# Seven products for seven of a layer's eight up blocks, with two of four weight sums made by accumulating transfers

## The chip, the cores and the metric

One NeuronCore of a Trainium2 chip runs the whole program. The metric is the device time of one execution in microseconds; lower is better. TensorE multiplies into PSUM, ScalarE and VectorE work on SBUF and PSUM, GpSimd (POOL) on SBUF, and the queues of SyncE (SP) and POOL start transfers from memory (HBM).

## The reference

A decoder trunk of two layers over 256 tokens with 2048 features, everything in float32. Each layer has an attention, a cross-attention into 256 memory tokens, and an MLP, each with an RMS norm ahead and a residual add behind. The change lies in the MLP, which is more than half of the work:

```python
def sq_relu_mlp(h, wup, wdown):
    return jnp.square(jax.nn.relu(h @ wup)) @ wdown        # wup 2048 x 8192, wdown 8192 x 2048

x = x + sq_relu_mlp(rms_norm(x, mlp_norm[i]), mlp_wup[i], mlp_wdown[i])
```

## The kernel before, in words

**Products.** TensorE takes float32 operands rounded to a shorter form, so each operand is kept as two parts, a high part and the rest, and each product is three matmuls: high by high, high by rest, rest by high. The activations stand still (128 x 128), the weights move (128 x 512). Activations are split once per layer stage, weights each time they are loaded.

**The path of a weight.** Weights come in tiles of 128 x 2048 floats (1024 KB) into one of RAWS = 6 raw buffers, by SP's queue. A tile is an item: `split_pieces` cuts it into two halves of 128 x 1024, ScalarE casts each to `whi` (L193), VectorE subtracts to get `wlo` (L194). whi and wlo have four buffers each, so two items' halves. TensorE then multiplies (all matmuls are recorded at L155). A raw buffer is free again when its second wlo is made; a whi or wlo buffer when TensorE has used that half.

**The MLP.** The hidden features come in eight blocks of 1024 (`MLP_BLOCKS`), each of two halves of 512. There are three kinds of item:

- an up item: one tile of `wup` by both token tiles (t = 0, 1), 24 matmuls of 512 columns; eight of them make a block;
- a down item: one tile of `wdown` by both token tiles, 24 matmuls, sums in PSUM that are added to the residual x at L439; four columns groups (c = 0 to 3) of two items for each block;
- a product item: one of the seven products of a block, half of its 16 row groups (x = 0, 1), 12 matmuls.

The seven products are Winograd's form of Strassen's rule for a 2 x 2 partition: the activations as a11 to a22 (token tile by half of the features), the block's weights as b11 to b22 (half of the features by half of the hidden columns). Seven products with sums of four forms of the activations (`s1` to `s4`, made once per layer by `Forms.sums`) and four sums of weight tiles take the place of eight. A block of up items has 2 x 4 x 24 = 192 matmuls, a block by seven products 14 x 12 = 168. Six blocks of a layer go by seven products (`SEVEN` = 1, 2, 3, 5, 6, 7), blocks 0 and 4 by up items.

`Seven.job` makes the weights of an item: it loads a tile, or adds tiles in raw buffers on VectorE at 128 x 2048 each. Before, the sums are p5 (L748, t = b12 - b11), p6 (L752, t = b22 - t), p7 (L757, t - b11) and p4 (L762, t - b21), each for x = 0 and 1, so eight a block. `Seven.products` multiplies, copies a finished product out of PSUM or adds it to another (`add`, L790, "evacuation" below), and passes the sums to `out`, which squares them on ScalarE, transposes them on TensorE and splits them for the down items.

**The order.** TensorE's order is written out: `mlp_line` mixes the items of seven products with the others (`rest`). It keeps a `lead`, the load of the items placed so far less their share by TensorE's time, and takes a product item where the lead is spent or a down item's hidden tiles are not there yet. The orders of VectorE, ScalarE, POOL and SP follow from a schedule that is made when the program is built; from then on each engine goes through its own fixed list, and waits in it. Loads are planned four items ahead (`AHEAD`), and a load waits in SP's list for its raw buffer.

Of the kernel before, what the change touches and what calls it, by code (L numbers as in the profile page):

```python
# [14 lines left out]
ALU = mybir.AluOpType  # L15
# [6 lines left out]
CH = 512  # L22
EPS = 1e-6
WARM = 13
RAWS = 6
MLP_BLOCKS = 8
SEVEN = (1, 2, 3, 5, 6, 7)
EVS = 7

T_EV, T_TURN, T_ROT, T_SM, T_SQ, T_ADD, T_NORM = 2.6, 2.6, 12.0, 6.5, 4.4, 2.2, 6.5  # L30
# [15 lines left out]
def trunk(ctx, tc, x, xT, mem, memT, positions, gcols, gfinal, lam_vecs, consts, W, out):  # L46
    nc = tc.nc

    def pool(name, bufs, space=None):
        kw = {"space": space} if space else {}  # L50
        return ctx.enter_context(tc.tile_pool(name=name, bufs=bufs, **kw))

    keep = pool("keep", 1)
    wraw = pool("wraw", RAWS)
    whalf = pool("whalf", 4)
    units = pool("units", 13)
    work = pool("work", 2)
    small = pool("small", 3)
    banks = pool("banks", 8, bass.MemoryType.PSUM)
# [104 lines left out]
    def load(dst, src, queue=None):  # L164
        tc.keep_in_program_order((queue or nc.sync).dma_start(dst, src))
# [4 lines left out]
    def raw_tile():  # L170
        return wraw.tile([P, 4 * CH], F32, tag="raw", name=nm("raw"))
# [25 lines left out]
    def halves_of(raw, n=4 * CH, pieces=2):  # L197
        split = split_pieces(raw, n, pieces)
        for _ in range(pieces):
            split.next()  # L200
        return split.halves
# [166 lines left out]
    class Forms(Stream):  # L368
# [34 lines left out]
        def sums(self):  # L403
            for key in [(t, h) for t in range(NT) for h in range(2)]:
                for task in self.forms[key].tasks:
                    yield task
            for x in range(2):
                a11, a12, a21, a22 = (self.raw[t][:, 8 * h + 4 * x : 8 * h + 4 * x + 4] for t in range(NT) for h in range(2))
                for key, o, p, q, op in (
                    ("s1", a22, a21, a22, ALU.add), ("s3", a21, a11, a21, ALU.subtract),  # L410
                    ("s2", a22, a22, a11, ALU.subtract), ("s4", a12, a12, a22, ALU.subtract),
                ):
                    nc.vector.tensor_tensor(o, p, q, op)
                    self.halves(key, x, o)
                yield T_TURN
# [290 lines left out]
    class Chunk:  # L706
# [11 lines left out]
        def items(self):  # L718
            return [Item(self, u, [job]) for u, job in enumerate(self.all)]
# [5 lines left out]
    class Seven:  # L725


        ORDER = "p1 p1 p5 p5 p6 p3 p6 p3 p7 p7 p2 p4 p2 p4".split()
        A = {"p1": (0, 0), "p2": (0, 1), "p3": "s4", "p4": (1, 1), "p5": "s1", "p6": "s2", "p7": "s3"}

        def __init__(self, l, b):
# [1 line left out]
            self.raw = {}  # L733
            self.banks = {}

        def fetch(self, i, j, x):
            raw = raw_tile()
            load(raw, W[f"mlp_wup{self.l}"][4 * (2 * self.b + j) + 2 * i + x])
            return raw

        def job(self, p, x):
            def run():
                r = self.raw
                if p == "p1":
                    r[11, x] = o = self.fetch(0, 0, x)
                elif p == "p5":
                    r["t", x] = o = self.fetch(0, 1, x)
                    nc.vector.tensor_tensor(o, o, r.pop((11, x)), ALU.subtract)  # L748
                elif p == "p6":
                    r[22, x] = self.fetch(1, 1, x)  # L750
                    o = r["t", x]
                    nc.vector.tensor_tensor(o, r[22, x], o, ALU.subtract)  # L752
                elif p == "p3":
                    o = r.pop((22, x))
                elif p == "p7":
                    o = self.fetch(0, 0, x)
                    nc.vector.tensor_tensor(o, r["t", x], o, ALU.subtract)  # L757
                elif p == "p2":
                    r[21, x] = o = self.fetch(1, 0, x)
                else:  # L760
                    o = r.pop(("t", x))
                    nc.vector.tensor_tensor(o, o, r.pop((21, x)), ALU.subtract)  # L762
                return halves_of(o)

            return run

        def items(self):
            order = [(p, self.ORDER[:i].count(p)) for i, p in enumerate(self.ORDER)]
            return [Item(self, u, [self.job(*u)]) for u in order]

        def products(self, a, u, copied, out):
            p, x = u
            form = a.form(self.A[p])
            need(form.tasks)
            if x == 0:
                self.banks[p] = bank("pr")
            o = self.banks[p]
            for h, (hi, lo) in enumerate(take()):
                for k in range(2):
                    kk = 4 * x + 2 * h + k  # L780
                    wh, wl = (w[:, k * CH : (k + 1) * CH] for w in (hi, lo))
                    mmul(o, form[:, 0, kk], wh, kk == 0, False)
                    mmul(o, form[:, 0, kk], wl, False, False)
                    mmul(o, form[:, 1, kk], wh, False, kk == 7)
                pump()
            if x == 0:
                return

            def add(o, p, q, op=ALU.add):
                nc.vector.tensor_tensor(o, p, q, op)  # L790

            c = copied
            if p in ("p1", "p5", "p6", "p3"):
                c[p] = work.tile([P, CH], F32, tag="ev", name=nm(p), bufs=EVS)
            if p in ("p1", "p5"):
                nc.scalar.copy(c[p], o)
            elif p == "p6":
                add(c[p], o, c["p1"])
            elif p == "p3":
                add(c[p], o, c["p5"])  # L800
                add(c[p], c[p], c["p6"])
                out(0, 1, c[p], c[p])
            elif p == "p7":
                add(c["p6"], o, c["p6"])
                add(c["p5"], c["p6"], c["p5"])
                out(1, 1, c["p5"], c["p5"])
            elif p == "p2":
                add(c["p1"], o, c["p1"])
                out(0, 0, c["p1"], c["p1"])
            else:  # L810
                add(c["p6"], c["p6"], o, ALU.subtract)
                out(1, 0, c["p6"], c["p6"])

    def mlp_line(l):

        def up(b, h):
            return Chunk(l, "up", [(b, h)]).items()

        def both(b, *more):
            return [(b, 0), (b, 1), *more]

        groups = [both(0), both(1, (4, 0)), both(2), both(3, (4, 1)), both(5), both(6), both(7)]

        def down(i):


            end = len(groups) - 1
            pairs = ((0, 1), (2, 3)) if (end - i) % 2 == 0 else ((2, 3), (0, 1))  # L830
            chunks = [Chunk(l, "down", groups[i], c, open=i in (0, 2)) for c in pairs[0]]
            chunks += [Chunk(l, "down", groups[i], c, close=i in (1, end)) for c in pairs[1]]
            return [i for c in chunks for i in c.items()]

        line = up(0, 0)
        rest = up(0, 1) + up(4, 0) + down(0) + down(1) + up(4, 1) + down(2) + down(3) + down(4) + down(5)
        seven = [i for b in SEVEN for i in Seven(l, b).items()]

        def vector(item):

            if isinstance(item.of, Seven):
                p, x = item.u
                return 2 + 2 * (p in ("p5", "p6", "p7", "p4")) + x * {"p6": 0.55, "p3": 1.65, "p7": 1.65, "p2": 1.1, "p4": 1.1}.get(p, 0)
            return 2 + 1.1 * (item.u == len(item.of.all) - 1 and item.of.close)

        def tensor(item):
            return 1 if isinstance(item.of, Seven) else 2

        rest, after = rest[:-3], rest[-3:]

        share = sum(map(vector, rest + seven)) / sum(map(tensor, rest + seven))
        usable = {(0, 0): 0}
        lead, now = 6.0, 0
        while rest or seven:
            of = rest[0].of if rest else None
            late = rest and of.kind == "down" and any(usable.get(h, math.inf) > now for h in of.halves)
            take_seven = seven and (not rest or late or lead <= 0)
            item = (seven if take_seven else rest).pop(0)
            lead += vector(item) - share * tensor(item)
            now += tensor(item)  # L860
            line.append(item)
            if isinstance(item.of, Seven):
                if item.u == ("p4", 1):
                    usable.update({(item.of.b, h): now + 6 for h in range(2)})
            elif item.of.kind == "up" and item.u == 3:
                usable[item.of.halves[0]] = now + 4
        return line + after, down(len(groups) - 1)
# [426 lines left out]
    down = mlp(1, norm, None)  # L1294
# [112 lines left out]
```

## Time and profile before

| | before |
|---|---|
| median of 3 runs | 2250.74 us (2250.48 to 2252.2) |
| the profiled execution | 2250.12 us, of which its span 2248.3 us |
| granted TensorE clock, mean | 0.999 |
| DVE busy | 1733.9 us |
| loads of `wup` | 152 of 1024 KB |
| sums of weight tiles on VectorE | 96 (24 each at L748, L752, L757, L762), about 2.29 us each |
| matmuls `pr` (seven products) | 2016 |

Layer 0's MLP lies between about 520 and 1175 us of the span, layer 1's between about 1580 and 2240. In the rows, PE is TensorE's matmuls and PEld its loads of standing operands, DVE is VectorE, ACT ScalarE; "out<-in" names the tiles, and the bracket or the last column says how long the engine stood idle before and what ended that. The mean time of a matmul in the rows (about 0.39 us) is longer than its pace, because matmuls overlap.

### The profile page before, as it was taken

How to read it: one execution, taken by the hardware profiler on the slowest of the kernel's cores; microseconds unless marked ns; L12 is line 12 of the kernel's file. 1: busy time of each engine (PE TensorE's matmuls, PEld its weight loads, DVE VectorE, ACT ScalarE, POOL GpSimd, SP SyncE). 2: the span in 40 equal slices, each digit the busy share in tenths (PEclk: the TensorE clock that was granted, in tenths of full speed). 3: DMA queues.
4: the chain of work that ended last, by engine and by line, in shares of the span. 5: the costliest groups of instructions: out<-in, count | busy, mean ns of one | idle time of the engine just before them, and what ended most of it. 6: DMA issues, size and time to landing. Idle time of an engine off the chain costs nothing.

```text
span 2248.3 us, 27367 instructions
## 1 busy us (share of the span) xinstructions
PE 2233.4 (99%) x10569; PEld 1862.0 (83%) x10569; DVE 1733.9 (77%) x1866; ACT 1338.1 (60%) x1787; POOL 104.7 (5%) x194
## 2 busy tenths in 40 slices
PE   9999999999999999999999999999999999999998
PEld 7888888888888888888889888888888888888886
DVE  6665747778888888888865766778888888888884
ACT  7544546666665666656655655566666566565664
POOL 0201010000000000000000311000000000000001
PEclk9999999999999999999999999999999999999999
DMA  9446555435666565656755334643565656566572
GB/s 364 168 136 220 195 189 198 167 123 215 208 222 229 190 245 199 242 206 219 249 177 182 110 141 150 243 150 133 223 233 193 247 197 241 200 223 225 208 279 75
DMA packets 69107, 450.52 MB, mean 200 GB/s; under 512 B 7921, under 2 KB 8305, under 8 KB 17521
## 3 DMA queue, kind: packets, MB, share of 16 engines
q1 hardware_dynamic: 68400, 447.73, 56.2%
q8 instruction: 82, 1.34, 0.2%
q10 hardware_dynamic: 576, 1.05, 0.1%
q14 instruction: 49, 0.39, 0.0%
HBM read 446.65 MB, written 2.10 MB: 200 GB/s over the span
## 4 chain that ended last, share of the span: by engine, by line
PE 93%; DVE 3%; issue 1%; ACT 1%; DMA 1%; ACTq 0%; POOLq 0%; DVEq 0%
PE mm L155 70%; PE pr L155 17%; PE ax L155 3%; PE ax L159 2%; DVE wlo L194 2%; PE mm L159 1%; ACT whi L193 1%; DMA raw<-in_mlp_wup_dram 1%; DVE raw L752 0%; DMA raw<-in_da_wqkv_dram 0%; DVE raw L748 0%; DVE raw L757 0%; DVE x L439 0%; ACT unit L315 0%; DVE unit L289 0%
## 5 line engine op out<-in xcount | busy, mean ns | idle before, releaser
L155 PE MATMUL mm<-whi,unit 128*128 128x512 f32 (+2 forms) x4800 | 1513.8, 388 | 1.0 <-ACT unit L572 0.9
L193 ACT CAST whi<-raw 128x1024 fp32r<-128x1024 f32 (+3 forms) x938 | 977.0, 1042 | 774.1 <-PE mm L155 639.6
L194 DVE TENSOR_TENSOR wlo<-raw,whi 128x1024 fp32r<-128x1024 f32 (+3 forms) x938 | 1123.4, 1210 | 401.2 <-ACT whi L193 385.5
L155 PEld LDWEIGHTS mm<-whi,unit 128*128 128x128 f32 x4800 | 897.0, 188 | 178.2 <-ACT unit L572 1.3
L155 PE MATMUL mm<-wlo,unit 128*128 128x512 f32 (+2 forms) x2400 | 926.5, 386 | 2.2 <-DVE wlo L194 1.6
L155 PEld LDWEIGHTS mm<-wlo,unit 128*128 128x128 f32 x2400 | 451.3, 188 | 90.8 <-DVE wlo L194 6.8
L155 PE MATMUL pr<-whi,unit 128*128 128x512 f32 x1344 | 436.7, 392 | 0.0
L155 PEld LDWEIGHTS pr<-whi,unit 128*128 128x128 f32 x1344 | 252.3, 188 | 51.8
L155 PE MATMUL pr<-wlo,unit 128*128 128x512 f32 x672 | 262.1, 390 | 0.5 <-DVE wlo L194 0.4
L155 PEld LDWEIGHTS pr<-wlo,unit 128*128 128x128 f32 x672 | 126.3, 188 | 27.5 <-DVE wlo L194 2.2
L439 DVE TENSOR_TENSOR x<-x,mm 128x512 f32<-128x512 f32 x152 | 100.5, 680 | 12.2 <-PE mm L155 11.5
L328 POOL TENSOR_TENSOR rs<-rs,mhalf 128x1 f32<-128x1 f32 (+1 forms) x28 | 23.5, 845 | 1268.8 <-DVE rs L327 1268.8
L748 DVE TENSOR_TENSOR raw<-raw,raw 128x2048 f32<-128x2048 f32 x24 | 54.9, 2286 | 9.1 <-DMA raw<-in_mlp_wup_dram 9.1
L288 ACT CAST unit<-ax 128x512 fp32r<-128x512 f32 (+1 forms) x88 | 48.8, 565 | 18.7 <-PE ax L159 16.0
L762 DVE TENSOR_TENSOR raw<-raw,raw 128x2048 f32<-128x2048 f32 x24 | 54.9, 2287 | 5.5 <-DMA raw<-in_mlp_wup_dram 5.3
L289 DVE TENSOR_TENSOR unit<-ax,unit 128x512 fp32r<-128x512 f32 (+1 forms) x88 | 57.3, 659 | 2.1 <-ACT unit L288 1.3
L752 DVE TENSOR_TENSOR raw<-raw,raw 128x2048 f32<-128x2048 f32 x24 | 54.9, 2286 | 4.9 <-DMA raw<-in_mlp_wup_dram 4.7
L757 DVE TENSOR_TENSOR raw<-raw,raw 128x2048 f32<-128x2048 f32 x24 | 54.9, 2286 | 3.2 <-DMA raw<-in_mlp_wup_dram 3.2
L501 ACT ACTIVATE p<-ax,nmax 128x256 f32<-128x256 f32 (+1 forms) x80 | 33.7, 429 | 30.0 <-DVE nmax L499 29.5
L322 ACT ACTIVATE junk<-x 128x512 bf16<-128x512 f32 x56 | 35.2, 628 | 9.4 <-DVE x L439 8.4
L159 PE MATMUL ax<-identr,p 128*128 128x128 f32 x272 | 40.7, 272 | 0.0
L159 PEld LDWEIGHTS ax<-identr,p 128*128 128x128 f32 x272 | 33.4, 139 | 8.3
(138 smaller groups left out, 998.1 us busy)
## 6 DMA issues: line engine op xcount, KB each, us to landing
raw<-in_mlp_wup_dram SPq DMA_DIRECT2D x152, 1024.0 KB, 4.9
raw<-in_mlp_wdown_dram SPq DMA_DIRECT2D x128, 1024.0 KB, 4.9
raw<-in_da_wqkv_dram SPq DMA_DIRECT2D x45, 1024.0 KB, 5.1
raw<-in_da_wo_dram SPq DMA_DIRECT2D x16, 1024.0 KB, 5.0
raw<-in_ca_wkv_dram SPq DMA_DIRECT2D x16, 1024.0 KB, 5.0
raw<-in_mla_wo_dram SPq DMA_DIRECT2D x16, 1024.0 KB, 5.0
raw<-in_ca_wq_dram SPq DMA_DIRECT2D x8, 1024.0 KB, 5.2
raw<-in_ca_wo_dram SPq DMA_DIRECT2D x8, 1024.0 KB, 5.0
```

The lines of the kernel that those rows point to most:

```text
L155: return nc.tensor.matmul(o, stationary, moving, start=start, stop=stop)
L159: nc.tensor.transpose(o, src, ident)
L193: nc.scalar.copy(hi, r)
L194: nc.vector.tensor_tensor(lo, r, f32(hi), ALU.subtract)
L288: nc.scalar.copy(hi, src)
L289: nc.vector.tensor_tensor(dst[:, 1, :n, t * P : (t + 1) * P], src, f32(hi), ALU.subtract)
L322: nc.scalar.activation(junk[:, : src.shape[1]], src, AF.Square, accum_out=acc)
L439: nc.vector.tensor_tensor(xc, xc, ps, ALU.add)
L748: nc.vector.tensor_tensor(o, o, r.pop((11, x)), ALU.subtract)
L752: nc.vector.tensor_tensor(o, r[22, x], o, ALU.subtract)
L757: nc.vector.tensor_tensor(o, r["t", x], o, ALU.subtract)
L762: nc.vector.tensor_tensor(o, o, r.pop((21, x)), ALU.subtract)
```

## The change

- Blocks 1 to 7 of each layer go by seven products (`SEVEN`), only block 0 by up items.
- The signs of two activation forms change (`s1` becomes a difference, `s4` a sum), and those of the results with them.
- Two of the four sums of weights are made by transfers: `fetch` with `onto` starts a load from POOL's queue that adds to what the tile holds. t = b12 + b11 is a plain load and an accumulating one (`sum`); p7's b22 + b12 is an accumulating load onto b22's tile, after p6 has used it. The other two stay on VectorE: p6's t = t + b22 (L765 of the changed file) and p2's t = t + b21 (L771), the latter used by p4. So VectorE has four sums a block, POOL four accumulating transfers.
- The order of the products is p1 p1 p3 p3 p5 p5 p6 p6 p2 p7 p2 p7 p4 p4; p3 is a plain tile and comes early.
- RAWS is 7, unit tiles are 12 instead of 13; p1, p3 and p5 are copied out of PSUM by ScalarE.
- The down items follow the blocks one by one; `vector` in `mlp_line` becomes `load`, with other weights for the items and a term for what transfers move, and the lead starts at 0.

```diff
-RAWS = 6
+RAWS = 7
-SEVEN = (1, 2, 3, 5, 6, 7)
+SEVEN = (1, 2, 3, 4, 5, 6, 7)
-    units = pool("units", 13)
+    units = pool("units", 12)
...
-                    ("s1", a22, a21, a22, ALU.add), ("s3", a21, a11, a21, ALU.subtract),
-                    ("s2", a22, a22, a11, ALU.subtract), ("s4", a12, a12, a22, ALU.subtract),
+                    ("s1", a22, a21, a22, ALU.subtract), ("s3", a21, a11, a21, ALU.subtract),
+                    ("s2", a22, a22, a11, ALU.subtract), ("s4", a12, a12, a22, ALU.add),
...
-        ORDER = "p1 p1 p5 p5 p6 p3 p6 p3 p7 p7 p2 p4 p2 p4".split()
+        ORDER = "p1 p1 p3 p3 p5 p5 p6 p6 p2 p7 p2 p7 p4 p4".split()
...
-        def fetch(self, i, j, x):
+        def fetch(self, i, j, x, onto=None):
+            src = W[f"mlp_wup{self.l}"][4 * (2 * self.b + j) + 2 * i + x]
+            if onto is not None:
+                tc.keep_in_program_order(nc.gpsimd.dma_start(onto, src, accum_op=ALU.add))
+                return onto
             raw = raw_tile()
-            load(raw, W[f"mlp_wup{self.l}"][4 * (2 * self.b + j) + 2 * i + x])
+            load(raw, src)
             return raw
+
+        def sum(self, x):
+            self.raw["t", x] = self.fetch(0, 1, x)
+            self.fetch(0, 0, x, self.raw["t", x])
 
         def job(self, p, x):
             def run():
                 r = self.raw
                 if p == "p1":
-                    r[11, x] = o = self.fetch(0, 0, x)
+                    o = self.fetch(0, 0, x)
+                    if x == 0:
+                        self.sum(x)
+                elif p == "p3":
+                    r[22, x] = o = self.fetch(1, 1, x)
+                    if x == 0:
+                        self.sum(1)
                 elif p == "p5":
-                    r["t", x] = o = self.fetch(0, 1, x)
-                    nc.vector.tensor_tensor(o, o, r.pop((11, x)), ALU.subtract)
+                    o = r["t", x]
                 elif p == "p6":
-                    r[22, x] = self.fetch(1, 1, x)
                     o = r["t", x]
-                    nc.vector.tensor_tensor(o, r[22, x], o, ALU.subtract)
-                elif p == "p3":
+                    nc.vector.tensor_tensor(o, o, r[22, x], ALU.add)
+                    self.fetch(0, 1, x, r[22, x])
+                elif p == "p7":
                     o = r.pop((22, x))
-                elif p == "p7":
-                    o = self.fetch(0, 0, x)
-                    nc.vector.tensor_tensor(o, r["t", x], o, ALU.subtract)
                 elif p == "p2":
-                    r[21, x] = o = self.fetch(1, 0, x)
+                    o = self.fetch(1, 0, x)
+                    nc.vector.tensor_tensor(r["t", x], r["t", x], o, ALU.add)
                 else:
                     o = r.pop(("t", x))
-                    nc.vector.tensor_tensor(o, o, r.pop((21, x)), ALU.subtract)
                 return halves_of(o)
...
-            if p in ("p1", "p5", "p6", "p3"):
+            if p in ("p1", "p3", "p5", "p6"):
                 c[p] = work.tile([P, CH], F32, tag="ev", name=nm(p), bufs=EVS)
-            if p in ("p1", "p5"):
+            if p in ("p1", "p3"):
                 nc.scalar.copy(c[p], o)
+            elif p == "p5":
+                nc.scalar.copy(c[p], o)
+                add(c["p3"], o, c["p3"])
             elif p == "p6":
                 add(c[p], o, c["p1"])
-            elif p == "p3":
-                add(c[p], o, c["p5"])
-                add(c[p], c[p], c["p6"])
-                out(0, 1, c[p], c[p])
+                add(c["p3"], c["p3"], c["p6"], ALU.subtract)
+                out(0, 1, c["p3"], c["p3"])
...
-        groups = [both(0), both(1, (4, 0)), both(2), both(3, (4, 1)), both(5), both(6), both(7)]
+        groups = [both(b) for b in range(MLP_BLOCKS)]
...
-        rest = up(0, 1) + up(4, 0) + down(0) + down(1) + up(4, 1) + down(2) + down(3) + down(4) + down(5)
+        rest = up(0, 1) + [i for b in range(MLP_BLOCKS - 1) for i in down(b)]
...
+                moved = {"p1": 3 - x, "p3": 2 - x, "p6": 1, "p2": 1}.get(p, 0)
+                added = x * {"p5": 0.55, "p6": 1.65, "p2": 1.1, "p7": 1.65, "p4": 1.1}.get(p, 0)
+                return 2 + 2 * (p in ("p6", "p2")) + added + moved
+            return 3 + 1.1 * (item.u == len(item.of.all) - 1 and item.of.close)
...
-        lead, now = 6.0, 0
+        lead, now = 0.0, 0
```

In block 2, TensorE's order becomes: p1, down, p1, down, p3, p3, p5, p5, p6, down, p6, down, down, p2, down, p7, p2, down, down, p7, p4, p4, in which the first of each pair is x = 0; blocks 3 and 4 have the same with other downs. In blocks 5 and 6 a down item stands between p3 and p5, and p6 follows p6 at once. In block 1, p3 p5 p5 p6 p6 follow each other, in block 7 p3 p5 p5 p6 p6 too.

More of the change, by code (lines that the diff above doesn't have):

```diff
@@ L792, in products @@
             c = copied
-            if p in ("p1", "p5", "p6", "p3"):
+            if p in ("p1", "p3", "p5", "p6"):
                 c[p] = work.tile([P, CH], F32, tag="ev", name=nm(p), bufs=EVS)
-            if p in ("p1", "p5"):
+            if p in ("p1", "p3"):
                 nc.scalar.copy(c[p], o)
+            elif p == "p5":
+                nc.scalar.copy(c[p], o)
+                add(c["p3"], o, c["p3"])
             elif p == "p6":
                 add(c[p], o, c["p1"])
-            elif p == "p3":
-                add(c[p], o, c["p5"])
-                add(c[p], c[p], c["p6"])
-                out(0, 1, c[p], c[p])
[L803 to L806, printed above, removed]
+                add(c["p3"], c["p3"], c["p6"], ALU.subtract)
+                out(0, 1, c["p3"], c["p3"])
             elif p == "p2":
@@ L809, in products @@
                 out(0, 0, c["p1"], c["p1"])
+            elif p == "p7":
+                add(c["p6"], o, c["p6"])
+                add(c["p5"], c["p5"], c["p6"], ALU.subtract)
+                out(1, 1, c["p5"], c["p5"])
             else:
-                add(c["p6"], c["p6"], o, ALU.subtract)
+                add(c["p6"], o, c["p6"])
                 out(1, 0, c["p6"], c["p6"])
@@ L830, in down, with load @@
             pairs = ((0, 1), (2, 3)) if (end - i) % 2 == 0 else ((2, 3), (0, 1))
-            chunks = [Chunk(l, "down", groups[i], c, open=i in (0, 2)) for c in pairs[0]]
-            chunks += [Chunk(l, "down", groups[i], c, close=i in (1, end)) for c in pairs[1]]
+            chunks = [Chunk(l, "down", groups[i], c, open=i == 0) for c in pairs[0]]
+            chunks += [Chunk(l, "down", groups[i], c, close=i == end) for c in pairs[1]]
             return [i for c in chunks for i in c.items()]
         line = up(0, 0)
-        rest = up(0, 1) + up(4, 0) + down(0) + down(1) + up(4, 1) + down(2) + down(3) + down(4) + down(5)
+        rest = up(0, 1) + [i for b in range(MLP_BLOCKS - 1) for i in down(b)]
         seven = [i for b in SEVEN for i in Seven(l, b).items()]
-        def vector(item):
+        def load(item):
             if isinstance(item.of, Seven):
                 p, x = item.u
-                return 2 + 2 * (p in ("p5", "p6", "p7", "p4")) + x * {"p6": 0.55, "p3": 1.65, "p7": 1.65, "p2": 1.1, "p4": 1.1}.get(p, 0)
-            return 2 + 1.1 * (item.u == len(item.of.all) - 1 and item.of.close)
+                moved = {"p1": 3 - x, "p3": 2 - x, "p6": 1, "p2": 1}.get(p, 0)
+                added = x * {"p5": 0.55, "p6": 1.65, "p2": 1.1, "p7": 1.65, "p4": 1.1}.get(p, 0)
+                return 2 + 2 * (p in ("p6", "p2")) + added + moved
+            return 3 + 1.1 * (item.u == len(item.of.all) - 1 and item.of.close)
         def tensor(item):
@@ L849, in mlp_line @@
         rest, after = rest[:-3], rest[-3:]
-        share = sum(map(vector, rest + seven)) / sum(map(tensor, rest + seven))
+        share = sum(map(load, rest + seven)) / sum(map(tensor, rest + seven))
         usable = {(0, 0): 0}
-        lead, now = 6.0, 0
+        lead, now = 0.0, 0
         while rest or seven:
@@ L858, in mlp_line @@
             item = (seven if take_seven else rest).pop(0)
-            lead += vector(item) - share * tensor(item)
+            lead += load(item) - share * tensor(item)
             now += tensor(item)
```

## The prediction

> **What bounds the kernel now.** I read the page's first part, then busy time by windows, then TensorE's waits inside the two MLP phases (they change, the rest does not), then what VectorE and ScalarE do just before those waits.
>
> ```profile
> span 2248.3 us, 27367 instructions
> PE 2233.4 (99%) x10569; PEld 1862.0 (83%) x10569; DVE 1733.9 (77%) x1866; ACT 1338.1 (60%) x1787; POOL 104.7 (5%) x194
> ```
>
> ```profile
> core 0: us, PE busy (x) PEld busy (x) DVE busy (x) ACT busy (x) POOL busy (x), PEclk, DMA share, GB/s
> 800.00:900.00 100.00, 99.73 (x450) 81.86 (x449) 85.65 (x75) 62.86 (x69) 0.00 (x0) 1.00 0.61 213
> 1800.00:1900.00 100.00, 99.85 (x449) 81.98 (x448) 85.78 (x77) 62.73 (x69) 0.00 (x0) 1.00 0.62 220
> ```
>
> TensorE sets the time. In an MLP stretch it is never free, VectorE has 14% left, ScalarE 37%, POOL does nothing, the transfers hold 0.61 of their engines. TensorE's waits, from 520 to 1200 us and then from 1560 to 2249:
>
> ```profile
> PE mm L155 <- DVE wlo L194: 0.9, 2, 0.7
> PE pr L155 <- DVE wlo L194: 0.2, 1, 0.2
> ```
>
> ```profile
> PE mm L155 <- DVE wlo L194: 0.2, 1, 0.2
> PE pr L155 <- DVE wlo L194: 0.2, 1, 0.2
> ```
>
> So all it ever waits for is VectorE's wlo, 1.5 us in all. The chain gives its pace:
>
> ```profile
> 784.73 5.44 PE mm L155 x24
> ```
>
> 0.2267 us for each 512-wide matmul: a product item of 12 takes 2.72, each of its halves 1.36, a down item 5.44.
>
> **What TensorE loses.** A block as eight up items has 192 matmuls, by seven products 168. One block in each layer changes over: 48 matmuls, 48 x 0.2267 = 10.9 us less. That is firm as long as TensorE is fed, and feeding it is the question.
>
> **How far ahead the splits may be.** whi and wlo have four buffers each, so the cast of a half waits until TensorE has used the half four back. That is the largest wait of the cast:
>
> ```profile
> ACT whi L193 <- PE mm L155: 639.6, 497, 2.9
> ```
>
> In a run of product items the casts therefore come every 1.36 us. Three of them, then VectorE and TensorE at the same place, where a sum began late:
>
> ```profile
> 674.05 1.06 ACT L193 CAST whi<-raw 128x1024 fp32r<-128x1024 f32 x1 [0.30 <-PE pr L155]
> 675.41 1.06 ACT L193 CAST whi<-raw 128x1024 fp32r<-128x1024 f32 x1 [0.30 <-PE pr L155]
> 676.77 1.06 ACT L193 CAST whi<-raw 128x1024 fp32r<-128x1024 f32 x1 [0.30 <-PE pr L155]
> ```
>
> ```profile
> 675.49 2.29 DVE L757 TENSOR_TENSOR raw<-raw,raw 128x2048 f32<-128x2048 f32 x1 [0.49 <-DMA raw<-in_mlp_wup_dram]
> 677.70 3.49 DVE L194 TENSOR_TENSOR wlo<-raw,whi 128x1024 fp32r<-128x1024 f32 x3
> ```
>
> ```profile
> 678.98 0.50 PE L155 MATMUL mm<-wlo,unit 128*128 128x512 f32 x1 [0.66 <-DVE wlo L194]
> ```
>
> A sum holds VectorE for 2.2 us (675.49 to 677.70), a wlo of 1.23 for (3.49 - 1.23) / 2 = 1.13. How long a buffer takes to come back, from the chain and from a matmul's mean time:
>
> ```profile
> 664.49 2.73 PE pr L155 x12
> 667.23 0.02 issue
> 667.25 1.06 ACT whi L193
> 668.32 0.02 issue
> 668.34 1.24 DVE wlo L194
> ```
>
> ```profile
> L155 PE MATMUL pr<-whi,unit 128*128 128x512 f32 x1344 | 436.7, 392 | 0.0
> ```
>
> From the half's end to the end of the wlo that reuses its buffer 669.58 - 667.22 = 2.36, and 0.392 - 0.227 = 0.17 for the last matmul to drain: 2.5 us. TensorE comes to that half's wlo three halves later, 4.08 + 0.23 = 4.3 us. So in a run of products VectorE can never be more than about 1.8 us ahead, however idle it was before; per half it gains only 1.36 - 1.13 = 0.23. One sum there is just too much, and the trace has that case (block 2's p1 p1 p5 p5):
>
> ```profile
> 652.79 2.28 DVE L752 TENSOR_TENSOR raw<-raw,raw 128x2048 f32<-128x2048 f32 x1
> 654.99 4.62 DVE L194 TENSOR_TENSOR wlo<-raw,whi 128x1024 fp32r<-128x1024 f32 x4
> ```
>
> ```profile
> 655.45 0.61 PE L155 MATMUL pr<-whi,unit 128*128 128x512 f32 x2
> 656.26 0.50 PE L155 MATMUL pr<-wlo,unit 128*128 128x512 f32 x1 [0.20 <-DVE wlo L194]
> ```
>
> The matmul due at 655.45 + 2 x 0.2267 = 655.90 came at 656.26: one sum in a run costs 0.36. By the slack, 2.2 - 1.8 - 0.23 = 0.2. I take 0.3.
>
> **What the new order does to that.** The change does what it says: the built program has 56 accumulating transfers and 56 sums. The sum for p6 is now t = t + r22, in place, so it can't start before p5 of the same x has been split; before, p5's sum had no such tie and was done early. And the order is p5 p5 p6 p6. In the built program VectorE's order in blocks 2, 3 and 4 of both layers is: p5x0's two wlo, p5x1 first, SUM for p6x0, p5x1 second, p6x0 first, SUM for p6x1, p6x0 second; TensorE runs p3 p3 p5 p5 p6 without a down item. The first sum costs 0.3. From p5x1's second wlo to p6x0's second, VectorE needs 1.13 + 2.2 + 1.13 = 4.46 and TensorE 2.72: 1.74 more, 2.0 us a block. The down item after p6x0 gives it all back to VectorE, but not to TensorE.
>
> Blocks 5 and 6 have a down item ahead of p5: the first sum is free and the second costs 0.2, but p6x1 follows at once, with an evacuation and a third sum (p2's, t + a21) between its two halves:
>
> ```profile
> 805.37 0.68 DVE L790 TENSOR_TENSOR p<-pr,p 128x512 f32<-128x512 f32 x1
> 805.97 1.21 DVE L194 TENSOR_TENSOR wlo<-raw,whi 128x1024 fp32r<-128x1024 f32 x1
> ```
>
> 0.6 for the evacuation, so 0.6 + 1.13 + 2.2 + 1.13 - 2.72 = 2.3, with the 0.2 2.5 a block. Block 1 has all three in one run: 0.3 + 1.74 + 2.3 = 4.4. Block 7 has two, and an evacuation before p6x1's first half (0.6 + 1.13 - 1.36 = 0.4): 2.4. A layer: 4.4 + 3 x 2.0 + 2 x 2.5 + 2.4 = 17.8; both, 35.6.
>
> **The rest of the change.** VectorE's work falls: 96 sums become 56 (40 x 2.29 = 92 us less), 24 more halves cost 24 x 1.13 = 27; evacuations stay at seven a block.
>
> ```profile
> L748 DVE TENSOR_TENSOR raw<-raw,raw 128x2048 f32<-128x2048 f32 x24 | 54.9, 2286 | 9.1 <-DMA raw<-in_mlp_wup_dram 9.1
> ```
>
> I cost that at nothing: VectorE is late for want of buffers, not of time. ScalarE gets 24 more casts and a third copy a block, under its 37% of spare. Flipped signs in the forms are the same instructions. A thirteenth unit tile goes, but a block's down items end before the block after next writes its hidden tiles. TensorE's present waits hang on sums that go; with the 0.36 - 0.20 that each hides, 1.5 + 5 x 0.16 = 2.3 us less.
>
> **The transfers.** A layer's MLP loads 140 tiles of 1024 KB now; then 128 on SP's queue and 28 accumulating ones on POOL's, which has nothing else to do there.
>
> ```profile
> q1 hardware_dynamic: 68400, 447.73, 56.2%
> ```
>
> ```profile
> raw<-in_mlp_wup_dram SPq DMA_DIRECT2D x152, 1024.0 KB, 4.9
> ```
>
> A 1024 KB tile (1.049 MB) holds all engines for 0.562 x 2248.3 x 1.049 / 447.73 = 2.96 us. The trace has no accumulating transfer; from below it is a plain load (2.96 and 4.9), and I bound it above by the cover. A new MLP phase has 2904 matmuls, 658 us; 128 x 2.96 = 379 leaves 279 for 28: they bind from 9.96 us each, 3.4 plain loads. Each waits for its own first load, or for the p6 sum that reads r22; behind it on POOL there are only the next ones, due later. The tightest in blocks 2 to 7 is t for x = 1: its load starts when p4x1's second half is split, some 0.8 us after TensorE began p4x1, and p5x1's cast wants the sum when p3x1's first half is done, p4x1, p1x0, down, p1x1, down, p3x0 and a half later: 4 x 2.72 + 2 x 5.44 + 1.36 - 0.8 = 22.3 us, less 4.9 for the load 17.4. Block 1 is tighter: r22 for x = 0 has p5x1, p6x0, p6x1 and half an up item less 0.6, 10.3 us after its sum, up to 14.7 with that block's stall. So up to some two or three plain loads of 4.9 it is hidden, and that is what I take. [...]
>
> What is near is p2x0's plain load in blocks 2 to 4. It takes the raw buffer of the down item before p6x1, so it starts on SP when that is split: VectorE is at p5x1's first wlo 2.8 us before TensorE is at p5x1 (4.1 - 1.3), and five wlo of 1.13, one of 1.23 and two sums on it is 8.5 us after. The load lands at 13.4. Its sum must start by 15.2, since with the 2.0 of stall TensorE is at the half behind it at 18.6, and 2.2 and 1.23 lie between. Beside an accumulating transfer the load may take longer, and later loads stand behind it. Six blocks by 0 to 1.5 us: 0 to 9. VectorE already waits for such loads now (9.1 us in the row of L748), so I keep 9 for the range and take 0.
>
> **The sum.** The profiled execution took 2250.12, 1.8 above its span and 0.6 below the median of 2250.74. 2250.1 - 10.9 - 2.3 + 35.6 = 2272.5, with the 0.6, 2273 us. 0.2% of this, 4.5 us, is what a measurement can tell from no change.
>
> **Rivals.**
> A, faster: the sums don't hold TensorE. It decides below 13.2 / 14 = 0.94 us a block. This would be so if VectorE entered p5 with more than four halves done, or if the sums ran beside TensorE's other delays. For it: VectorE has less to do than now, and only 1.5 us of waits come from the present 96 sums. Against it: the buffers are four, and 656.26 shows one sum already costing. With 0 to 0.36 a block, 2237.5 to 2242.5: 2240. Chance 0.14; for within 0.2% (stalls of 9 to 18 us) 0.04.
> B, much slower: the accumulating transfers bind. From 3.4 plain loads on; at four, 28 x 11.84 + 379 = 711 a layer, 53 us over TensorE's 658, so 2250.7 - 13.2 + 106 = 2343. For it: a price that nothing here shows. Against it: 0.61 of the engines are used now, and 3.4 is far above the plain load. [...] Chance 0.14.
> Forecast: 0.68.
>
> **How the numbers follow.** The forecast's own range is 2264 (three quarters of the stalls) to 2284 (with late p2x0 loads and a little more). To leave out no more than 0.2, the range goes down to 2258, without reaching A, and up to 2302 into the mild end of B. Faster 0.14, same 0.04, slower 0.68 + 0.14 = 0.82.
>
> **What would show it.** Right: 2016 + 336 pr matmuls; TensorE's waits for wlo up from 1.5 to about 30 us, in some 14 places of 1.5 to 2 us just after p5x1, each behind a 128x2048 sum; p7's and p5's splits not waiting for POOL's transfers; DMA share at 0.7 to 0.85. Wrong: TensorE's waits under 10 us (then A); or the share near 1, with casts waiting for transfers (then B); or accumulating transfers landing after more than 17 us.

## The result, and the profile after

The changed kernel took 2291.07 us (median of 4 runs, 2288.52 to 2295.6), the kernel before 2250.77 on the same chip: ratio 1.018, 95% interval 1.0162 to 1.0198, 40 us slower. 2273 was forecast, in a range of 2258 to 2302.

The page's first part, then busy time in the two stretches that were shown of before (us, busy time and count of each engine, granted clock, share of the DMA engines, GB/s):

```profile
span 2288.3 us, 27494 instructions
PE 2232.9 (98%) x10521; PEld 1851.6 (81%) x10521; DVE 1686.3 (74%) x1864; ACT 1363.0 (60%) x1829; POOL 153.8 (7%) x250
```

```profile
800.00:900.00 100.00, 95.84 (x432) 78.33 (x431) 77.47 (x71) 61.21 (x68) 3.58 (x5) 1.00 0.79 242
1800.00:1900.00 100.00, 95.73 (x426) 77.94 (x425) 79.82 (x71) 62.42 (x68) 4.40 (x5) 1.00 0.69 213
```

TensorE has 48 matmuls fewer and is still longer on its way: in the two stretches where it was 99.7 and 99.9% busy it is now at 95.8 and 95.7%. VectorE has less to do than before (77.5 for 85.7 in the first stretch) and is what TensorE waits for. The waits from 520 to 1220 us, layer 0's MLP (us in all, times, longest):

```profile
DVE raw L771 <- DMA raw<-in_mlp_wup_dram: 22.4, 10, 5.0
PE pr L155 <- DVE wlo L194: 13.0, 8, 1.7
PE mm L155 <- DVE wlo L194: 6.9, 3, 2.5
```

And from 1590 to 2289 us, layer 1's:

```profile
DVE raw L771 <- DMA raw<-in_mlp_wup_dram: 22.3, 10, 5.1
PE pr L155 <- DVE wlo L194: 13.0, 8, 1.7
PE mm L155 <- DVE wlo L194: 7.3, 3, 2.5
```

Eleven stops a layer, of two kinds. The eight at `pr` are the forecast's: a product item waits for a wlo that stands behind a sum. Block 2's, VectorE first, then TensorE:

```profile
645.41 2.28 DVE L765 TENSOR_TENSOR raw<-raw,raw 128x2048 f32<-128x2048 f32 x1
647.61 3.48 DVE L194 TENSOR_TENSOR wlo<-raw,whi 128x1024 fp32r<-128x1024 f32 x3
```

```profile
646.68 0.61 PE L155 MATMUL pr<-whi,unit 128*128 128x512 f32 x2
648.88 0.50 PE L155 MATMUL pr<-wlo,unit 128*128 128x512 f32 x1 [1.59 <-DVE wlo L194]
```

The matmul due at 646.68 + 2 x 0.2267 = 647.13 came at 648.88. The three at `mm`, in blocks 2, 3 and 4, are longer and have another cause. p2's sum (L771) stands on VectorE between the two halves of a down item and waits for p2x0's load. SP's issue of that load, VectorE, TensorE:

```profile
651.12 0.33 SPq L165 DMA_DIRECT2D raw<-in_mlp_wup_dram  x1
```

```profile
660.14 2.29 DVE L771 TENSOR_TENSOR raw<-raw,raw 128x2048 f32<-128x2048 f32 x1 [4.77 <-DMA raw<-in_mlp_wup_dram]
662.35 2.35 DVE L194 TENSOR_TENSOR wlo<-raw,whi 128x1024 fp32r<-128x1024 f32 x2
```

```profile
663.62 0.50 PE L155 MATMUL mm<-wlo,unit 128*128 128x512 f32 x1 [2.21 <-DVE wlo L194]
```

The load went out at 651.12 and landed at about 660.1, after 9.0 us. It ran beside two accumulating transfers, which POOL issued at 643.66 and, as soon as the sum at 645.41 was done, at 648.34; the row of a stretch in between shows the 16 DMA engines full (1.01):

```profile
648.34 0.88 POOL L740 DMA_DIRECT2D raw<-in_mlp_wup_dram  x1 [3.81 <-DVE raw L765]
```

```profile
650.00:655.00 5.00, 5.00 (x24) 4.14 (x23) 4.81 (x5) 2.11 (x2) 0.00 (x0) 1.00 1.01 205
```

What such a transfer takes follows from the page's rows of the queues and of the issues (the last number of an issue is the median time to landing):

```profile
q1 hardware_dynamic: 64944, 422.56, 51.2%
q0 software_dynamic: 8064, 58.72, 13.5%
```

```profile
raw<-in_mlp_wup_dram SPq DMA_DIRECT2D x128, 1024.0 KB, 5.7
raw<-in_mlp_wup_dram POOLq DMA_DIRECT2D x56, 1024.0 KB, 10.3
```

An accumulating tile holds all engines for 0.135 x 2288.3 / 56 = 5.5 us, a plain one for 0.512 x 2288.3 x 1.049 / 422.56 = 2.9: 1.9 plain loads.

### The profile page after: what moved, and what is told of

It is laid out like the page before. It is cut to its first block, busy times and chain, and to the rows that moved or that the text cites. A ratio compares the mean times of both kernels' runs of the same rounds, so it can differ in the third digit from the quotient of the medians.

```text
span 2288.3 us, 27494 instructions
## 1 busy us (share of the span) xinstructions
PE 2232.9 (98%) x10521; PEld 1851.6 (81%) x10521; DVE 1686.3 (74%) x1864; ACT 1363.0 (60%) x1829; POOL 153.8 (7%) x250
## 3 DMA queue, kind: packets, MB, share of 16 engines
q1 hardware_dynamic: 64944, 422.56, 51.2%
## 4 chain that ended last, share of the span: by engine, by line
PE 87%; DVE 7%; DMA 3%; issue 2%; ACT 2%; ACTq 0%; POOLq 0%; DVEq 0%
PE mm L155 64%; PE pr L155 17%; DVE wlo L194 4%; PE ax L155 3%; DMA raw<-in_mlp_wup_dram 2%; PE ax L159 2%; DVE raw L765 2%; ACT whi L193 1%; PE mm L159 1%; DVE raw L771 0%; DMA raw<-in_da_wqkv_dram 0%; DVE x L439 0%; ACT unit L315 0%; DVE unit L316 0%; DVE unit L488 0%
## 5 line engine op out<-in xcount | busy, mean ns | idle before, releaser
L194 DVE TENSOR_TENSOR wlo<-raw,whi 128x1024 fp32r<-128x1024 f32 (+2 forms) x962 | 1153.8, 1210 | 453.6 <-ACT whi L193 436.0
L193 ACT CAST whi<-raw 128x1024 fp32r<-128x1024 f32 (+2 forms) x962 | 995.6, 1041 | 755.4 <-PE mm L155 612.2
L155 PE MATMUL mm<-whi,unit 128*128 128x512 f32 (+3 forms) x4544 | 1434.7, 389 | 1.3 <-ACT unit L572 0.9
L155 PEld LDWEIGHTS mm<-whi,unit 128*128 128x128 f32 x4544 | 849.7, 188 | 168.7 <-ACT unit L572 1.3
L155 PE MATMUL mm<-wlo,unit 128*128 128x512 f32 (+3 forms) x2272 | 877.3, 386 | 15.0 <-DVE wlo L194 15.0
L155 PE MATMUL pr<-whi,unit 128*128 128x512 f32 x1568 | 505.9, 392 | 0.0
L155 PE MATMUL pr<-wlo,unit 128*128 128x512 f32 x784 | 309.7, 395 | 27.8 <-DVE wlo L194 26.0
L740 POOL DMA_DIRECT2D raw<-in_mlp_wup_dram x56 | 49.4, 882 | 1120.7 <-DVE wlo L194 390.5
L771 DVE TENSOR_TENSOR raw<-raw,raw 128x2048 f32<-128x2048 f32 x28 | 64.1, 2290 | 44.6 <-DMA raw<-in_mlp_wup_dram 44.6
L765 DVE TENSOR_TENSOR raw<-raw,raw 128x2048 f32<-128x2048 f32 x28 | 64.0, 2285 | 0.1
L801 DVE TENSOR_TENSOR p<-pr,p 128x512 f32<-128x512 f32 x70 | 47.8, 682 | 0.0
## 6 DMA issues: line engine op xcount, KB each, us to landing
raw<-in_mlp_wup_dram POOLq DMA_DIRECT2D x56, 1024.0 KB, 10.3
```

Source lines behind the costliest of these rows:

```text
L155: return nc.tensor.matmul(o, stationary, moving, start=start, stop=stop)
L193: nc.scalar.copy(hi, r)
L194: nc.vector.tensor_tensor(lo, r, f32(hi), ALU.subtract)
L740: tc.keep_in_program_order(nc.gpsimd.dma_start(onto, src, accum_op=ALU.add))
L765: nc.vector.tensor_tensor(o, o, r[22, x], ALU.add)
L771: nc.vector.tensor_tensor(r["t", x], r["t", x], o, ALU.add)
```

## Experiments

The theory: (1) sums on VectorE stand too close together for the four buffers of halves and stop TensorE, the `pr` stops; (2) p2x0's load, started late and slowed by accumulating transfers, is behind the `mm` stops. The rivals: that the accumulating transfers hold the kernel as a whole, or that one of the two causes carries all of it. All kernels were timed beside the kernel before.

### Without p6's sums

```diff
-                    nc.vector.tensor_tensor(o, o, r[22, x], ALU.add)
```

> Leaves out the 28 sums t = t + r22 ahead of p6 (p6, p2 and p4 then use another weight); all transfers, the accumulating ones too, and the order stay. Sums theory (two sums inside four halves stop TensorE): the eleven stops a layer of TensorE for wlo go but for some tenths, and because VectorE reaches the down item before p6x1 some 4 us sooner, p2x0's load is on time too: 2291 - 39 - 15 = 2237, up to 2245 with single sums of p2 that still cost 0.3 each. Transfers theory (the accumulating transfers and their traffic hold the kernel): nothing of the traffic changes, so 2280 or more.

2238.78 us, 0.9945 of before (0.993 to 0.9959): 52 us less than the changed kernel, with all its transfers. TensorE's groups (busy, mean ns, then idle time before them and what ended it):

```profile
L155 PE MATMUL mm<-wlo,unit 128*128 128x512 f32 (+3 forms) x2272 | 876.3, 386 | 1.1 <-DVE wlo L194 0.7
L155 PE MATMUL pr<-wlo,unit 128*128 128x512 f32 x784 | 305.9, 390 | 0.5
```

Both kinds of stop are gone. That rules out the transfers as a bound on the whole, but doesn't part the two causes, since VectorE also reaches the later load's place sooner.

### Without the accumulating transfers, and with plain ones in their place

The first leaves the call out, the second keeps it as a copy:

```diff
-                tc.keep_in_program_order(nc.gpsimd.dma_start(onto, src, accum_op=ALU.add))
```

```diff
-                tc.keep_in_program_order(nc.gpsimd.dma_start(onto, src, accum_op=ALU.add))
+                tc.keep_in_program_order(nc.gpsimd.dma_start(onto, src))
```

> Leaves out the 56 accumulating transfers (t and r22 keep only their first load); both sums on VectorE and the order stay. Sums theory: the stops of 1.6 to 1.7 us just after p5x1 stay (13.0 us a layer for the products), and only the stops of 2.2 to 2.5 us behind p2's sum (7 us a layer), which waits for a late load, go if it is the traffic that makes that load late: 2291 - 15 = 2276. Transfers theory: nearly all of it goes, 2237 to 2250.

> The 56 transfers on POOL's queue copy where they added, into the same tiles from the same weights, so the sums a11 + a12 and a22 + a12 are not formed; all else stays. This parts the number of bytes from the adding. If an accumulating transfer holds the engines for nearly two plain loads and p2x0's load is late for that, the transfers land in about 5 to 6 us, the stops of 2.2 to 2.5 us behind p2's sum mostly go, as without these transfers: 2275. If the added traffic alone makes it late: within 5 us of the changed kernel, 2286 to 2291. The stops of 1.6 us after p5x1 stay in both.

2273.48 us (1.0097, 1.008 to 1.0113) and 2273.15 us (1.0099, 1.0082 to 1.0116). TensorE's groups and p2's sum without the transfers (its line is L770 there):

```profile
L155 PE MATMUL mm<-wlo,unit 128*128 128x512 f32 (+3 forms) x2272 | 876.1, 386 | 0.0
L155 PE MATMUL pr<-wlo,unit 128*128 128x512 f32 x784 | 309.7, 395 | 27.6 <-DVE wlo L194 25.7
L770 DVE TENSOR_TENSOR raw<-raw,raw 128x2048 f32<-128x2048 f32 x28 | 64.1, 2290 | 14.1 <-DMA raw<-in_mlp_wup_dram 14.0
```

With plain transfers on the same queue, the queue's row, the issues' and TensorE's group:

```profile
q0 software_dynamic: 8064, 58.72, 7.1%
```

```profile
raw<-in_mlp_wup_dram POOLq DMA_DIRECT2D x56, 1024.0 KB, 6.3
```

```profile
L155 PE MATMUL mm<-wlo,unit 128*128 128x512 f32 (+3 forms) x2272 | 875.6, 385 | 0.2 <-DVE wlo L194 0.2
```

The `mm` stops go in both, the `pr` stops stay (25.7 against 26.0 us). The same packets and bytes as copies hold the engines for 0.071 x 2271.2 / 56 = 2.9 us each and land in 6.3, and then no load stops TensorE, though p2's sums still wait 21.9 us for theirs (44.6 in the changed kernel). So it is the adding, not the number of transfers, that makes p2x0's load late, and it costs 18 us.

### One weight buffer more

```diff
-RAWS = 7
+RAWS = 8
-    units = pool("units", 12)
+    units = pool("units", 11)
```

> One weight buffer more (8 for 7), one hidden tile fewer (11 for 12) to make room. Late start theory for the stops of 2.2 to 2.5 us behind p2's sum: its load waits for a buffer, so that with a buffer more it starts an item sooner and lands in time; these stops go and VectorE's wait for loads ahead of p2's sums falls from 44.6 us to under 15, while the 1.6 us stops after p5x1 stay: 2291 - 15 = 2276. Slow transfer theory (the load is slow beside the accumulating ones, wherever it starts): under 5 us gained. If the hidden tile is missed, stops appear ahead of the splits of hidden tiles and the time rises.

2277.18 us (1.0114, 1.0099 to 1.0129), 14 less than the changed kernel.

```profile
L155 PE MATMUL mm<-wlo,unit 128*128 128x512 f32 (+3 forms) x2272 | 876.0, 386 | 0.0
L155 PE MATMUL pr<-wlo,unit 128*128 128x512 f32 x784 | 310.0, 395 | 31.0 <-DVE wlo L194 29.1
L771 DVE TENSOR_TENSOR raw<-raw,raw 128x2048 f32<-128x2048 f32 x28 | 64.0, 2287 | 3.4 <-DMA raw<-in_mlp_wup_dram 3.4
```

p2's sums wait 3.4 us for loads instead of 44.6, with the accumulating transfers in place (landing in 10.0). The load is late only because it is both started late and slowed; taking away either is enough to spare TensorE. The `pr` stops grow by 3 us.

### A down item ahead of each sum

```diff
-            take_seven = seven and (not rest or late or lead <= 0)
+            due = seven and not late and seven[0].u[0] in ("p6", "p2") and isinstance(line[-1].of, Seven)
+            take_seven = seven and (not rest or late or not due and lead <= 0)
```

> Everything of the changed kernel kept, only the order of the line altered: a down item is put ahead of each item that has a sum (p6 and p2) where one is usable. Sums theory: in blocks 2 to 7 no two sums stand within four halves, so that single sums of 0 to 0.4 us are left and block 1's run (2.6 us): some 4.5 us a layer, 2291 - 54 + 9 = 2246, or 2261 if p2x0's loads stay as late as they are. Transfers theory: the same bytes in the same time, 2280 or more.

2280.65 us (1.0132, 1.0116 to 1.0147): a miss by 20 us and more. The waits of the whole span:

```profile
DVE raw L771 <- DMA raw<-in_mlp_wup_dram: 38.5, 16, 4.5
PE mm L155 <- DVE wlo L194: 24.9, 8, 3.9
PE pr L155 <- DVE wlo L194: 2.0, 4, 0.6
```

Theory (1) holds: the `pr` stops fall from 26.0 to 2.0 us. But the late loads cost more, 24.9 us for 14.2, in stops of up to 3.9 us: each of the eight stands behind a p2 sum that waited for its load. The expectation had allowed at most what they cost in the changed kernel. What they cost beyond the stops is in the last section.

The same order with eight weight buffers and eleven hidden tiles takes away both:

> The order with a down item ahead of each sum where one is usable, together with eight weight buffers and eleven hidden tiles. The order alone left no stop after p5x1 but stops of 3 to 4 us behind p2's late loads, with a lower granted clock behind them; the buffer alone took the late loads away. If the two causes are separate and complete, both go: 2237 and some 5 to 9 for single sums and block 1, 2242 to 2246, faster than the kernel before. If the closer order makes the transfers bind, the late loads return elsewhere: 2260 or more.

2239.5 us (0.9952, 0.9937 to 0.9967), 2.5 us below what was expected of two separate causes. TensorE's groups:

```profile
L155 PE MATMUL mm<-wlo,unit 128*128 128x512 f32 (+3 forms) x2272 | 876.8, 386 | 0.0
L155 PE MATMUL pr<-wlo,unit 128*128 128x512 f32 x784 | 306.5, 391 | 2.0 <-DVE wlo L194 1.2
```

So each edit takes away one of the two kinds of stop. Their gains don't add, 10 and 14 us alone and 52 together, because the order without the buffer makes the late loads later.

### Five buffers for halves

```diff
-    whalf = pool("whalf", 4)
-    units = pool("units", 12)
+    whalf = pool("whalf", 5)
+    units = pool("units", 11)
```

> Five buffers for the split halves where there are four, one hidden tile fewer (11). Window theory: VectorE may be one half (1.36 us) further ahead, so the stops of 1.6 us fall to some 0.3 to 0.6, and the stops of blocks 5 to 7 by as much; 13 runs of two or three sums save 1.36 each, about 2 x 9 = 18 to 24 us; p2's load also starts with VectorE, not sooner against TensorE: 2267 to 2273, down to 2255 if the late loads gain the same 1.36 six times and their own stops shrink. Rival (VectorE or the transfers are simply out of time in these stretches): within 5 us of 2291.

2250.13 us (0.9992, 0.9983 to 1.0002), 41 us less, more than either end of what was expected.

```profile
L155 PE MATMUL mm<-wlo,unit 128*128 128x512 f32 (+3 forms) x2272 | 876.1, 386 | 2.2 <-DVE wlo L194 2.1
L155 PE MATMUL pr<-wlo,unit 128*128 128x512 f32 x784 | 306.4, 391 | 7.2 <-DVE wlo L194 7.2
L771 DVE TENSOR_TENSOR raw<-raw,raw 128x2048 f32<-128x2048 f32 x28 | 64.1, 2288 | 32.8 <-DMA raw<-in_mlp_wup_dram 32.4
```

The `pr` stops fall from 26.0 to 7.2 us: the window is the limit, as the forecast had it, since VectorE's work is the same. The loads are still late (32.4 us for p2's sums), but VectorE is a half further ahead and TensorE hardly sees it: `mm` 2.1.

The kernel before with a fifth buffer, and the changed kernel's own order with both buffers, ask what of this belongs to the change:

> The kernel before, with five buffers for the halves and twelve hidden tiles in place of four and thirteen. If what the last kernel gained over the kernel before comes from the 48 fewer products once nothing holds TensorE, this one gains only what the kernel before still waits: 0 to 3 us, 2248 to 2251. If the fifth buffer is worth something of its own in every stretch: 2240 to 2246.

> The changed kernel's own order with eight weight buffers, five for halves and ten hidden tiles. Sums theory: with the fifth half a pair of sums still costs a few tenths and block 1 about 2, and the late loads are gone: 3.6 us a layer of waits for the products are left, 2240 to 2246. If the order matters beyond that (p2's sum next to p6's), 2247 or more; if it doesn't matter at all with these buffers, 2233 to 2237 as with the other order.

The kernel before gains 5.5 us: 2245.2 (0.9972, 0.9962 to 0.9982), the second of the two expectations. The fifth buffer has a worth of its own; the stretch from 800 to 900 us, where TensorE was 99.73 busy, is now full:

```profile
800.00:900.00 100.00, 100.00 (x454) 82.78 (x453) 84.55 (x75) 62.94 (x70) 0.00 (x0) 1.00 0.61 217
```

The changed order with both buffers took 2255.84 (1.0019, 1.001 to 1.0028), 10 us above what the theory of the sums expected and 6 above the kernel with five halves alone. It is the case that was named for 2247 or more, that the order matters beyond the two causes. TensorE's waits for products there, in layer 0, and a new wait of ScalarE:

```profile
PE pr L155 <- DVE wlo L194: 7.3, 5, 1.8
ACT unit L288 <- PE mm L155: 8.3, 5, 1.7
```

The split of a hidden tile now waits for one of the ten. That row fits a split that falls later, among the sums; but neither that nor p2's sum next to p6's, the reason named beforehand, was tested by itself, so why the `pr` stops double (14.5 us in all for 7.2) stays open.

### Order and both buffers

> As the one before it, with five buffers for halves too and ten hidden tiles. What is left of block 1's run (2.6 us a layer) and of single sums goes: 2238 to 2241. If ten hidden tiles are too few, the splits of hidden tiles wait for down items and TensorE for them: 2245 or more.

2234.55 us (2232.95 to 2235.16), 0.9926 of before (0.9911 to 0.994), the fastest of all, some 3 us below what was expected, 16 below the kernel before and 56 below the changed kernel:

```profile
span 2231.2 us, 27489 instructions
```

```profile
L155 PE MATMUL mm<-wlo,unit 128*128 128x512 f32 (+3 forms) x2272 | 875.6, 385 | 0.3 <-DVE wlo L194 0.3
L155 PE MATMUL pr<-wlo,unit 128*128 128x512 f32 x784 | 305.2, 389 | 0.0
```

Ten hidden tiles are not too few in this order. Against the kernel before with five halves, which VectorE doesn't hold up either (0.0 us idle ahead of TensorE's two wlo groups), it is 10.7 us faster.

## Why the prediction was right, and where its size was off

**The range.** The forecast's own range was 2264 to 2284, and 2291 lies above it. It lies in the part up to 2302 that was added for the mild end of rival B, which did not come true. That the whole range held was luck in this respect; the direction and the main cost were not.

**The 48 matmuls, 10.9 us.** Borne out: with VectorE holding up TensorE on neither side the difference is 2245.2 - 2234.55 = 10.7 us, or 11.1 when each is set against the kernel before that was timed beside it.

**The sums, 35.6 us.** Right in kind and place. Foretold were some 14 stops of 1.5 to 2 us just after p5x1; there are 16 `pr` stops of 1.56 to 1.70 us (block 2's is above; block 1 has two). From start to start of layer 0's matmuls, block 1 loses 4.5 us (4.4 forecast), blocks 2 to 4 about 2.2 each (2.0), blocks 5 and 6 2.7 each (2.5), block 7 2.55 (2.4): 19.1 for 17.8, and in layer 1 the same: 38.2 for 35.6 in all. The reason given, four buffers and not VectorE's time, is shown by the fifth buffer.

**The waits that go, 2.3 us.** Too small: counted the same way, from start to start, TensorE loses 3.3 and 2.7 us in the two MLPs of the kernel before, 6.0 in all, because shorter delays, of 0.24 and 0.11 us at 635.77 and 636.11 for one, stand in no row of waits. The kernel before with five halves has none of them and gains 5.5. So two errors, 2.6 us too little for the sums and 3.7 too little here, offset each other: 2250.7 - 10.9 - 6.0 + 38.2 = 2272.0, where the runs without adding took 2273. That these meet the forecast so closely is luck too.

**p2x0's load, 0 to 9, taken as 0.** This is the step that failed, the mis-sized term. The forecast named the place, the blocks, and a margin of 15.2 - 13.4 = 1.8 us. The margin was right: the load took 9.0 us where 4.9 had been put in, 4.1 more, less 1.8 gives 2.3, and the six stops are 2.2 to 2.5. What was wrong is the load's time beside accumulating transfers: the range allowed stops of at most 1.5 us, which is a load of 4.9 + 1.8 + 1.5 = 8.2, and the sum allowed nothing. The runs without adding put its worth at 18 us, the run with an eighth buffer at 14. Without it the kernel takes 2273.

**The accumulating transfers as such.** Hidden, as forecast: no cast in either MLP waited for a transfer, all 56 landed in time for p5 and p7 at a median of 10.3 us, against the 17.4 that the tightest of blocks 2 to 7 has. They hold 1.9 plain loads, where they would bind from 3.4; the DMA share is 0.69 to 0.80 in stretches of 100 us of the MLPs (0.7 to 0.85 forecast). Why an accumulating transfer holds the engines for 5.5 us, where the same bytes as a copy hold them for 2.9, is not shown by these runs. The forecast worked a longer time, up to some three plain loads, through to the accumulating tiles alone, and put nothing into the sum for the plain load that runs beside two of them.

**Rival A** decided below 0.94 us a block and would have meant 2240; the stops were 2.2 to 4.5 a block. The changed work with another order and one more weight buffer does land there (2239.5): what A had as the outcome is within reach of the change, but not with its order and buffers. **Rival B** fell: the transfers hold single loads, not the kernel.

**What was costed at nothing.** VectorE's smaller work (1686.3 for 1733.9 us) did not keep TensorE from stopping, as forecast. ScalarE's added casts and copies and the missing thirteenth hidden tile stand behind none of TensorE's waits in the two MLPs.

## What to carry to other kernels

VectorE was busy for 74% of the changed kernel's span and stopped TensorE for 40.2 us in its MLPs (13.0 + 6.9 + 13.0 + 7.3). So for an engine that feeds the one that sets the pace, count by how many buffers it may run ahead, and set the longest run of its work inside that window against the pace, not against its share of the span. A transfer that is itself in time made another one late: beside two accumulating ones, which stopped no cast, a plain load took 9.0 us, for a median of 4.9 in the kernel before. For each load beside such a transfer, set the margin against the time that the load takes in company. And where two causes overlap, take each away alone and both together; here 10 and 14 us alone were 52 together.

## What was not expected of the hardware

In these runs TensorE's granted clock was lower behind some of its stops, down to 0.50. In the kernel with a down item ahead of each sum, a stop of 2.79 us and the stretches around it (the number before the last two is the granted clock):

```profile
742.00:745.00 3.00, 0.39 (x2) 0.00 (x0) 3.00 (x2) 1.04 (x1) 0.00 (x0) 1.00 0.87 180
745.00:748.00 3.00, 2.82 (x7) 2.24 (x8) 3.00 (x4) 0.00 (x0) 0.00 (x0) 0.58 0.64 172
748.00:751.00 3.00, 3.00 (x12) 2.38 (x12) 0.86 (x2) 1.08 (x2) 0.00 (x0) 0.85 0.42 178
```

```profile
745.18 0.58 PE L155 MATMUL mm<-wlo,unit 128*128 128x512 f32 x1 [2.79 <-DVE wlo L194]
745.57 1.05 PE L155 MATMUL mm<-whi,unit 128*128 128x512 f32 x2
746.42 0.63 PE L155 MATMUL mm<-wlo,unit 128*128 128x512 f32 x1
```

Matmuls come every 0.43 us (745.57, 746.42) instead of 0.2267. In the rows from 745 to 751 the clock lacks 3 x (0.42 + 0.15) = 1.7 us, which makes 3.4 us at half rate. Six of that kernel's seven stops of 2.8 us and more have such a stretch at their end: five of some 3.4 us and one of 6.8, at the stop of 3.80 us that ends at 1818.16. For two of the five, behind the stops that end at 1096.62 and 2167.48, this is an estimate from the starts of their matmuls: nine take 3.64 us and eleven 4.10, 1.6 us more than at 0.2267 each. The one that ends at 658.15, of 3.38 us, has none. Its mean granted clock is 0.993, that of the changed kernel 0.998, where only one of the six stops over 2 us has it (0.57 from 664 to 668). A stretch of 3.4 us at half rate loses 1.7, so that the stop of 2.79 us cost more than half its length again, which no sum of waits shows; in that kernel some 12 us, an estimate from these stretches (5 x 1.7 + 3.4 = 11.9). This is part of why that order alone gained so little. The length of the stop alone doesn't decide it: one of 2.21 us had it (663.62 in the changed kernel) and one of 2.79, while one of 3.38 had none. What decides is not settled by these runs.
